# Softmax over rows of 1024: which queue issues each store

## The chip, the cores and the metric

The kernel runs on one core of a Trainium2 chip. The metric is the device time of one execution in microseconds (us). The kernel before takes 317.09 us, the median of three runs (316.88 to 317.21).

The core has several engines, each with an instruction queue of its own. VectorE (DVE in the profile) does reductions and elementwise arithmetic, ScalarE (ACT) the exponentials, GpSimd (POOL) next to nothing here, and SyncE (SP) only issues transfers. ACT, Pool and SP can all issue a DMA transfer between the chip's main memory (HBM) and the on-chip memory (SBUF). Each of the three has a DMA queue, which the profile calls q10, q0 and q1; the transfers of all three are carried by the same 16 DMA engines.

## The reference

The input x is 32 x 512 x 1024 in float32, so 16384 rows of 1024 numbers; `temperature` is 0.5. Each row goes through a softmax:

```
scaled = x / temperature
shifted = scaled - np.max(scaled, axis=-1, keepdims=True)
exp_x = np.exp(shifted)
return exp_x / np.sum(exp_x, axis=-1, keepdims=True)
```

Input and output are 67.11 MB each, and each is moved once.

## The kernel before

The rows are cut into 11 tiles. In a tile every one of the 128 partitions holds k whole rows of 1024 numbers side by side: k is 11 for tile 0, 12 for tiles 1 to 9 and 9 for tile 10 (`PASSES`, line 10). A transfer of a tile moves 128 pieces, one per partition, of 44 to 48 KB (36 KB for tile 10). Within a tile the rows are worked on in groups: 4, 4 and 3 in tile 0, two groups of 6 in each of tiles 1 to 9, and 4, 3 and 2 in tile 10. That makes 24 groups.

Each group goes through these steps, all in place in the tile:

- `maximum` (line 63): DVE takes the maximum of each row (line 69) and turns it into a bias (line 72).
- `exponential` (line 74): ACT computes exp of the scaled and shifted row, one instruction per row, and sums it as it goes (line 78).
- `divide` (line 87): DVE takes the reciprocal of the sums (line 90) and multiplies. In tiles 2, 3, 4, 6 and 8 (`WHOLE`) one instruction does the whole group (line 93), in the others there is one instruction per row (line 96).
- `store` (line 100): after the last group of a tile, the whole tile is sent to HBM by one transfer (line 108), and the next load is issued (line 109, line 60).

The order is written out by hand (`manual_schedule`, line 113): the instructions of each engine stand in its queue in the order in which the loop emits them. For each group g the loop emits its maximum and its exponentials, and then the divide and the store of group g - 1. So on DVE the divide of a group stands behind the maximum of the next group, and on ACT a store stands behind the exponentials of the next group. From tile 9 on (`ALONE`), the first group of a tile is preceded by the divide and the store of the group before.

There are four buffers for tiles (`BUFS`). Four loads are issued at the start, all by SP, and the load of tile i + 4 has to wait until the store of tile i has landed. All loads are on SP's queue, in order.

The stores of tiles 0 to 5 are issued by Pool and those of tiles 6 to 10 by ACT (`BY_POOL`, line 107). Ahead of the store of tile 0, Pool copies one column of tile 2 into a small tile `seen` that nothing reads (line 106). That copy waits for the load of tile 2, so the first store is issued only after this load has landed.

Of the kernel before, what the change touches and what calls it, by code (L numbers as in the profile page):

```python
# [1 line left out]

# [4 lines left out]

PASSES = [[4, 4, 3]] + [[6, 6]] * 9 + [[4, 3, 2]]  # L10
BUFS = 4

WHOLE = (2, 3, 4, 6, 8)


BY_POOL = 6

ALONE = 9


@with_exitstack
def kernel(
    ctx: ExitStack,
    tc: tile.TileContext,
    x: bass.AP,
    temperature: bass.AP,
    out: bass.AP,
):
    nc = tc.nc
    f32 = mybir.dt.float32  # L30
    scale = 1.0 / float(temperature)
    extreme = mybir.AluOpType.max if scale > 0 else mybir.AluOpType.min

    P = 128
    xf = x.flatten_outer_dims()
    of = out.flatten_outer_dims()
    n, d = xf.shape
    rows = [sum(ks) for ks in PASSES]
    assert sum(rows) * P == n

    data = ctx.enter_context(tc.tile_pool(name="data", bufs=BUFS))
    stats = ctx.enter_context(tc.tile_pool(name="stats", bufs=4))


    groups = []
    for i, ks in enumerate(PASSES):
        for j, k in enumerate(ks):
            groups.append((i, sum(ks[:j]), k))

    def dram(t, i):  # L50
        block = t[P * sum(rows[:i]) : P * sum(rows[: i + 1]), :]
        return block.rearrange("(p k) d -> p k d", p=P, k=rows[i])

    tiles, small = [], []

    def load():
        i = len(tiles)
        if i < len(PASSES):
            xt = data.tile([P, rows[i], d], f32, name="xt")
            nc.sync.dma_start(out=xt, in_=dram(xf, i))  # L60
            tiles.append(xt)

    def maximum(g):
        i, a, k = groups[g]
        top, bias, sums, recip = (
            stats.tile([P, k], f32, name=name) for name in ("top", "bias", "sums", "recip")
        )
        small.append((bias, sums, recip))
        nc.vector.tensor_reduce(  # L69
            out=top, in_=tiles[i][:, a : a + k, :], axis=mybir.AxisListType.X, op=extreme  # L70
        )
        nc.vector.tensor_scalar_mul(bias, in0=top, scalar1=-scale)  # L72

    def exponential(g):
        i, a, k = groups[g]
        bias, sums, _ = small[g]
        for b in range(k):
            nc.scalar.activation(  # L78
                tiles[i][:, a + b, :],
                tiles[i][:, a + b, :],  # L80
                mybir.ActivationFunctionType.Exp,
                bias=bias[:, b : b + 1],
                scale=scale,
                accum_out=sums[:, b : b + 1],
            )

    def divide(g):
        i, a, k = groups[g]
        _, sums, recip = small[g]
        nc.vector.reciprocal(recip, sums)  # L90
        if i in WHOLE:
            xt = tiles[i][:, a : a + k, :]
            nc.vector.tensor_mul(xt, xt, recip.unsqueeze(2).to_broadcast([P, k, d]))  # L93
            return
        for b in range(k):
            nc.vector.tensor_scalar_mul(  # L96
                tiles[i][:, a + b, :], in0=tiles[i][:, a + b, :], scalar1=recip[:, b : b + 1]
            )

    def store(g):  # L100
        i, a, k = groups[g]
        if a + k == rows[i]:
            if i == 0:


                nc.gpsimd.tensor_copy(stats.tile([P, 1], f32, name="seen"), tiles[2][:, 0, 0:1])  # L106
            queue = nc.gpsimd if i < BY_POOL else nc.scalar
            queue.dma_start(out=dram(of, i), in_=tiles[i])  # L108
            load()

    with tc.manual_schedule():
        for _ in range(BUFS):
            load()
        for g in range(len(groups) + 1):

            alone = g < len(groups) and groups[g][0] >= ALONE and groups[g][1] == 0
            if g > 0 and alone:
                divide(g - 1)  # L120
                store(g - 1)
            if g < len(groups):
                maximum(g)
                exponential(g)
            if g > 0 and not alone:
                divide(g - 1)
                store(g - 1)


# [1 line left out]
_INS = ['x', 'temperature']  # L131
_OUTS = [((32, 512, 1024), 'float32')]

_NUMBERS = {'temperature': 0.5}


# [26 lines left out]
```

## Time and profile before

| | us |
|---|---|
| median of three timed runs | 317.09 |
| span of the profiled execution, first to last instruction | 316.0 |
| DVE busy | 257.3 (81%) |
| ACT busy | 148.4 (47%) |
| POOL busy | 3.7 (1%) |
| one load of 6144 KB, issue to landing (median) | 36.4 |
| one store of 6144 KB by Pool, issue to landing (median) | 36.6 |
| one store of 6144 KB by ACT, issue to landing (median) | 33.1 |
| store of tile 10 (4608 KB) by ACT, issue to landing | 14.1 |

The profile shows one execution. The only time it gives for that execution is its span; the 1.1 us between the span and the median lie outside the first and the last instruction. Times within the profile count from the start of the span. Lines of the timeline give start, length, engine, line, operation, output and input; the bracket at the end tells how long the engine was idle before and what ended that. A letter q behind an engine's name (ACTq, SPq) marks its queue at the moment it issues a transfer; the length there is that of the issue, not of the transfer. Lines of the chain give start, length and what was worked on. DMA share and GB/s are those of the 16 DMA engines together; a packet counts where it starts, so short stretches scatter around the true rate.

### The profile page before, as it was taken

The numbers are of one execution on the slowest core, as the hardware profiler recorded it, in microseconds if no ns is written. First come the engines' busy times: TensorE is split into PE (matmuls) and PEld (weight loads), VectorE is DVE, ScalarE is ACT, GpSimd is POOL, SyncE is SP. The second block draws the span as 40 slices with busy tenths as digits, with TensorE's granted clock in tenths as the row PEclk, the third lists the DMA queues.
The fourth block names the chain that finished last, engine by engine and source line by source line (L and its number), as shares of the span: only waits on it lengthen the run. The fifth ranks groups of instructions, "written<-read, shape, count | busy, mean of one in ns | idle before, by whom it ended". The sixth has DMA issues, their size and how long they took to land.

```text
span 316.0 us, 529 instructions
## 1 busy us (share of the span) xinstructions
DVE 257.3 (81%) x150; ACT 148.4 (47%) x257; POOL 3.7 (1%) x11
## 2 busy tenths in 40 slices
DVE  0099999999999699979949993997399999888900
ACT  0048477468174444717181771447154705916600
POOL 0000010000000000000000000000000000000000
DMA  9999999999999999999999999999999999999995
GB/s 365 402 460 398 473 423 370 394 468 396 485 404 411 485 398 429 468 404 454 436 404 473 417 404 479 411 412 473 411 423 460 411 448 420 428 478 417 398 465 238
DMA packets 3171, 134.24 MB, mean 425 GB/s; under 512 B 352, under 2 KB 352, under 8 KB 352
## 3 DMA queue, kind: packets, MB, share of 16 engines
q1 hardware_dynamic: 1584, 67.11, 49.7%
q0 software_dynamic: 864, 37.22, 27.2%
q10 hardware_dynamic: 720, 29.88, 21.9%
q14 instruction: 3, 0.02, 0.0%
HBM read 67.11 MB, written 67.11 MB: 425 GB/s over the span
## 4 chain that ended last, share of the span: by engine, by line
DMA 47%; DVE 29%; ACT 10%; issue 9%; DVEq 0%; SPq 0%; POOLq 0%
DMA xt<-in_x_dram 24%; DMA out_dram<-xt 23%; DVE top L69 17%; ACT xt L78 10%; DVE xt L96 9%; DVE xt L93 2%; DVE bias L72 1%; DVE recip L90 0%; DVEq L158 0%; SPq L60 0%; POOLq L108 0%
## 5 line engine op out<-in xcount | busy, mean ns | idle before, releaser
L78 ACT ACTIVATE xt<-xt,bias 128x1024 f32<-128x1024 f32 x128 | 145.2, 1135 | 134.4 <-DVE recip L90 73.2
L69 DVE TENSOR_REDUCE top<-xt 128x6 f32<-128x6144 f32 (+3 forms) x24 | 140.1, 5836 | 36.9 <-DMA xt<-in_x_dram 36.9
L93 DVE TENSOR_TENSOR xt<-xt,recip 128x6144 f32<-128x6144 f32 x10 | 65.6, 6558 | 0.6 <-DVE recip L90 0.2
L96 DVE TENSOR_SCALAR xt<-xt,recip 128x1024 f32<-128x1024 f32 x68 | 46.3, 749 | 0.5
L78 ACT ACTIVATION_READ_ACCUMULATOR xt<-xt,bias 128x1 f32 x128 | 23.9, 186 | 0.0
L78 ACT ACT_TABLE_LOAD x1 | 1.3, 1283 | 16.4 <-DMA xt<-in_x_dram 16.4
L90 DVE RECIPROCAL recip<-sums 128x6 f32<-128x6 f32 (+3 forms) x24 | 4.3, 181 | 4.8 <-ACT xt L78 4.8
L108 POOL DMA_DIRECT2D out_dram<-xt x6 | 3.3, 555 | 128.9 <-ACT xt L78 83.7
L72 DVE TENSOR_SCALAR bias<-top 128x6 f32<-128x6 f32 (+3 forms) x24 | 4.1, 171 | 0.8
L106 POOL COPY seen<-xt 128x1 f32<-128x1 f32 x1 | 0.2, 185 | 45.0 <-DMA xt<-in_x_dram 45.0
L144 POOL MEMSET const-bfloat16-1.0<- 128x1 bf16 x1 | 0.1, 102 | 0.0
L144 POOL MEMSET const-uint8-127<- 128x1 uint8 x1 | 0.1, 102 | 0.0
L144 POOL MEMSET const-float32-0.0<- 128x1 f32 x1 | 0.1, 99 | 0.2 <-issue 0.2
L144 POOL MEMSET const-float32-1.0<- 128x1 f32 x1 | 0.1, 99 | 0.0
## 6 DMA issues: line engine op xcount, KB each, us to landing
xt<-in_x_dram SPq DMA_DIRECT2D x9, 6144.0 KB, 36.4
out_dram<-xt POOLq DMA_DIRECT2D x5, 6144.0 KB, 36.6
out_dram<-xt ACTq DMA_DIRECT2D x4, 6144.0 KB, 33.1
xt<-in_x_dram SPq DMA_DIRECT2D x1, 5632.0 KB, 15.6
out_dram<-xt POOLq DMA_DIRECT2D x1, 5632.0 KB, 29.2
xt<-in_x_dram SPq DMA_DIRECT2D x1, 4608.0 KB, 36.3
out_dram<-xt ACTq DMA_DIRECT2D x1, 4608.0 KB, 14.1
```

What stands on the lines that cost most here:

```text
L69: nc.vector.tensor_reduce(out=top, in_=tiles[i][:, a : a + k, :], axis=mybir.AxisListType.X, op=extreme)
L72: nc.vector.tensor_scalar_mul(bias, in0=top, scalar1=-scale)
L78: nc.scalar.activation(tiles[i][:, a + b, :], tiles[i][:, a + b, :], mybir.ActivationFunctionType.Exp, bias=bias[:, b : b + 1], scale=scal ...
L90: nc.vector.reciprocal(recip, sums)
L93: nc.vector.tensor_mul(xt, xt, recip.unsqueeze(2).to_broadcast([P, k, d]))
L96: nc.vector.tensor_scalar_mul(tiles[i][:, a + b, :], in0=tiles[i][:, a + b, :], scalar1=recip[:, b : b + 1])
L106: nc.gpsimd.tensor_copy(stats.tile([P, 1], f32, name="seen"), tiles[2][:, 0, 0:1])
L108: queue.dma_start(out=dram(of, i), in_=tiles[i])
L144: nc = _bacc.Bacc("TRN2", target_bir_lowering=False, num_devices=1)
```

## The change

Only the choice of the queue for each store changes, and the copy goes away. ACT issues the stores of tiles 0, 2, 4, 6 and 10, Pool those of tiles 1, 3, 5, 7, 8 and 9. The store of tile 0 is issued by ACT, without Pool's copy of a column of tile 2 ahead of it. Loads, groups, arithmetic and buffers are as before.

```diff
-BY_POOL = 6
+BY_POOL = (1, 3, 5, 7, 8, 9)
...
     def store(g):
         i, a, k = groups[g]
         if a + k == rows[i]:
-            if i == 0:
-
-
-                nc.gpsimd.tensor_copy(stats.tile([P, 1], f32, name="seen"), tiles[2][:, 0, 0:1])
-            queue = nc.gpsimd if i < BY_POOL else nc.scalar
+            queue = nc.gpsimd if i in BY_POOL else nc.scalar
             queue.dma_start(out=dram(of, i), in_=tiles[i])
             load()
```

## The prediction

> **What bounds the kernel now.** I read the page's busy row first, then its slices, then the stretches of the trace.
>
> ```profile
> span 316.0 us, 529 instructions
> DVE 257.3 (81%) x150; ACT 148.4 (47%) x257; POOL 3.7 (1%) x11
> DMA  9999999999999999999999999999999999999995
> q1 hardware_dynamic: 1584, 67.11, 49.7%
> q0 software_dynamic: 864, 37.22, 27.2%
> q10 hardware_dynamic: 720, 29.88, 21.9%
> ```
>
> The DMA row has no slice below nine tenths but the last: the 16 DMA engines are the bound. Queue q1 is SP's (loads), q0 Pool's, q10 ACT's. The stretches say how fast they go (start and end, length, DVE, ACT, POOL busy, then DMA share and GB/s):
>
> ```profile
> 16.00:46.00 30.00, 29.20 (x23) 18.28 (x30) 0.18 (x1) 1.00 0.97 421
> 46.00:48.00 2.00, 2.00 (x1) 2.00 (x5) 0.67 (x1) 1.00 0.92 393
> 48.00:50.00 2.00, 2.00 (x1) 0.58 (x2) 0.00 (x0) 1.00 1.54 393
> 50.00:52.00 2.00, 1.93 (x6) 1.41 (x3) 0.00 (x0) 1.00 0.78 338
> 52.00:60.00 8.00, 8.00 (x6) 5.49 (x10) 0.00 (x0) 1.00 0.93 401
> 100.00:200.00 100.00, 85.41 (x36) 47.39 (x84) 1.60 (x3) 1.00 1.00 433
> 200.00:300.00 100.00, 88.16 (x63) 51.70 (x90) 0.00 (x0) 1.00 1.00 433
> 312.00:316.00 4.00, 0.00 (x0) 0.00 (x0) 0.00 (x0) 1.00 0.13 55
> ```
>
> Saturated, they move 433 GB/s. The 134.22 MB need 310.0 us of that. SP issues at 0.74, the last store lands at 300.94 + 14.1 = 315.0, so at most some 5 us of 316.0 can be won. The only dip after the start is around 48 to 52, when the first store begins. In the packet records (8 packets per engine and transfer, 1.81 us each, 1.67 for tile 0) all 16 packets of load 3 that begin at 48.3 to 48.8 take 2.9 to 3.15 us, one 4.08: a **pause** of 1.2 us on 15 engines and 2.3 on one. Pool's first packets follow at 51.3. The engine with 4.08 ends last of all, at 314.74; the others end at 313.0 to 314.0, which is the thin last stretch, 312 to 316.
>
> The timeline shows the issues that the change touches:
>
> ```profile
> 45.46 0.18 POOL L106 COPY seen<-xt 128x1 f32<-128x1 f32 x1 [45.02 <-DMA xt<-in_x_dram]
> 46.04 0.67 POOL L108 DMA_DIRECT2D out_dram<-xt  x1 [0.39 <-issue]
> 65.86 0.53 POOL L108 DMA_DIRECT2D out_dram<-xt  x1 [19.16 <-DVE xt L96]
> ...
> 208.80 1.10 ACTq L108 DMA_DIRECT2D out_dram<-xt  x1
> 237.10 0.34 ACTq L108 DMA_DIRECT2D out_dram<-xt  x1
> 300.94 0.34 ACTq L108 DMA_DIRECT2D out_dram<-xt  x1
> ```
>
> And the chain shows the tail: load 8 lands at 226.1, and from there DVE and ACT work without a gap to the last divide.
>
> ```profile
> 187.96 38.14 DMA xt<-in_x_dram
> 226.09 0.02 issue
> 226.12 6.56 DVE top L69
> ...
> 282.21 4.34 DVE top L69
> ...
> 299.49 0.75 DVE xt L96
> ```
>
> The last store's first packet leaves at 302.4, when tile 9's store ends. SP's first load took 1.0 us from issue to first packet (0.74 to 1.73), so the issue at 300.94 is only about 0.5 us early.
>
> **The change part by part.** Bytes, loads and all DVE and ACT arithmetic stay; 11 stores stay 11. Pool issues six (0.53 each) before and after, ACT five (1.10 the first, 0.34 the others).
>
> *The copy (0.18 us at 45.46) and store 0 on ACT.* Pool loses a copy and the 0.39 gap: off the path, zero. Tile 0's last divide ends at 43.84; Pool issued at 46.04. ACT's queue holds six exponentials of tile 1 ahead of the store, which run to 48.6. That the issue can run ahead of queued exponentials is seen at 237.10, where two more start later (237.46, 238.59). Bounds: 43.9 to 48.6 for the issue, so 2.2 us earlier to 2.5 later. I take 46, as before: nine instructions are still queued at 43.84, five were at 237.10. What waits behind the store on ACT is tile 1's second group, released by DVE at 50.6, so neither the wait nor the first issue's 1.10 us costs anything. DMA is covered either way by load 3 (queued, landing at about 71). On SP, load 4 waits for store 0 (issued at 75.31); the store shifts it by at most the same 2.5 us while store 1 keeps the engines full. Without that cover each us would count in full. Zero.
>
> *The pause.* It goes with a store's first start. Three readings: it belongs to the first write of all (it stays, with store 0), to Pool's queue being used first (it moves to store 1, issued at 65.86), or to any start of Pool's queue from empty. Before, that happened once: stores 1 to 5 were appended to a busy q0, and 100:200, with three such issues, ran at 433. An empty q10 was first used at 208.80 with no dip (433 in 200:300). Bounds: it vanishes, -1.9 (below), or it comes at four starts, at stores 1, 3, 5 and 7 (8 and 9 are appended), +3.6 to +6.8. I take one pause, the single count that the trace shows: -1.2 + 1.2 = 0.
>
> *Stores 1 to 7 alternate.* The order of transfers could change now, since two stores may share the engines with a load. From issue to landing the trace gives 29.2, 34.7, 36.8, 36.6, 36.6, 41.4, 35.4 us for stores 0 to 6, so each next store is issued 9.4, 7.7, 7.5, 7.5, 10.4, 10.0 and 7.1 us before the one ahead lands. A store on an empty queue needs time to its first packet: 5.2 (store 0), 6.3 (store 6, beside two queues), 3.8 (load 4, beside one). The last packet ends 1 to 4 us before the landing. So the stores would meet for 0 to 3 us, and store 6 after store 5, already on another queue, met it for none: it started at 215.07, where q0 ended at 214.85. Work is conserved: at 98.4, where store 1's packets ended, stores 0 and 1 are done in both kernels with the same share of load 4. Bounds: from half a packet gained for loads (-0.9) to one packet lost (+1.81). I take zero, by the nearest row, store 6.
>
> *Stores 7, 8 and 9 from ACT to Pool.* Pool's issue has no queue ahead of it; ACT's came at the end of the divide too (237.10, 257.57, 282.24). ACT loses 3 x 0.34 us, idle time. 8 and 9 are queued behind a running store for 14 and 7 us. Zero.
>
> The row that bears on Pool's part is DVE's: right after 65.86, 122.15, 177.39, 237.10 and 257.57 it runs reductions of 6.5 us each, after 282.24 of 7.9, not divides. The Trainium skill (SBUF — State Buffer, "SBUF: two separate sides") warns that descriptors of a Pool-issued DMA can't be written while DVE runs a two-port operation, and recommends ACT's or SP's queue. By that rule alone, as an estimate, a start would wait for up to one divide run (4.07 us, L96), and with each of four Pool starts exposed the time would be 333; by the row the cost is zero, since reductions follow each issue and loads fill the wait.
>
> *Store 10* stays on ACT; store 9 ahead of it is now on another queue. It was queued before store 9 ended; now it interleaves with it, and the same bytes end together. Zero, at most +1.0 if its start is late by that first-packet time.
>
> Sum against the profiled execution: 316.0 + 0 = 316.0. The median, 317.09, is 1.1 above this span; I take that as unchanged: **317.1**.
>
> **The rivals.**
>
> *Pool's queue pauses at each start.* Place: stores 3, 5 and 7, beside store 1. Price 1.2 each on a saturated engine: +3.6, 320.7; if one engine were hit by 2.3 each time, +6.8, 323.9. For it: only Pool's queue showed a pause at a start; q10 and q1 (79.1) started from empty without. Against: one instance, and it was also the first write. It decides from the second pause on. Chance 0.27.
>
> *The pause goes away.* All engines end 1.2 earlier and the straggler no longer lags: the end falls from 314.74 to 313.98 - 1.2 = 312.8, so -1.9, 315.2. For it: queues ACT and SP have none. Against: Pool's queue still has its first use, at store 1. Chance 0.20. If it stays but hits all engines alike, the end is 313.98: -0.8, 316.3; chance 0.06.
>
> *Stores run ahead of loads.* If at stores 4 and 5 (10.4 us of early issue, the largest) a store takes one packet's turn from the loads and gives none back, load 8 lands 1.81 later, the gapless tail moves with it, and after 0.5 of slack the end is 1.3 later: 318.4. It decides from 0.5 us. Against: the gap after each store hands the turns back. Chance 0.09.
>
> *It does not do what it says:* store 0 waits for the exponentials and leaves at 48.6, later than Pool's. Price zero, as above; it is inside the forecast.
>
> **How the numbers follow.** Forecast 0.38: 317.1, own range 316.4 to 317.9, of which 0.30 within 0.2% (0.63 us, about what a measurement of this kernel can tell), 0.04 each side. Faster: 0.20 + 0.06 + 0.04 = 0.30. Slower: 0.27 + 0.09 + 0.04 = 0.40. The range reaches the case without a pause, 315.2 less 0.4 for a fully even end, and the case of four pauses with one uneven hit, 320.7 + 1.1: 314.8 to 321.8.
>
> **What would show it.** q0 with 864 packets and 37.75 MB, q10 720 and 29.36 MB; no copy on Pool; store 0 issued by ACT between 43.9 and 48.6. One dip below 433 GB/s in 46 to 80 and none in 100:300 is the forecast; dips near 127, 182 and 242 are the first rival; no dip the second. Load 8 landing later than 226.6 is the third. Wrong also if SP's loads wait for more than before: load 4 issued later than 78, with a stretch in 68 to 90 below 425.

## The result, and the profile after

The changed kernel takes 320.42 us (median of six runs, 319.49 to 322.55) against 317.15 for the kernel before: a ratio of 1.0109 (95% interval 1.008 to 1.0137). It is slower by about 1.1%, and its runs scatter over 3 us where those of the kernel before lie within 0.5. In the larger series beside the experiments the kernel before scatters too: of 29 runs beside runs 5 to 7 most lie near 317.3, and six between 318.8 and 320.3.

The page of the changed kernel, its busy row, its slices and its queues:

```profile
span 318.0 us, 525 instructions
DVE 257.3 (81%) x150; ACT 148.5 (47%) x257; POOL 3.5 (1%) x10
DMA  9999998999999999999999999999999999999976
q1 hardware_dynamic: 1584, 67.11, 49.5%
q0 software_dynamic: 864, 37.75, 27.5%
q10 hardware_dynamic: 720, 29.36, 21.4%
```

The arithmetic is the same to 0.1 us, and the queues carry just the bytes that were foreseen. What is new stands at the end of the DMA row: 7 and 6 instead of 9 and 5. Stretches (start and end, length, DVE, ACT, POOL busy, DMA share, GB/s) of the kernel before:

```profile
46.00:60.00 14.00, 13.93 (x10) 9.48 (x18) 0.67 (x1) 1.00 0.99 390
100.00:200.00 100.00, 85.41 (x36) 47.39 (x84) 1.60 (x3) 1.00 1.00 433
200.00:300.00 100.00, 88.16 (x63) 51.70 (x90) 0.00 (x0) 1.00 1.00 433
300.00:304.00 4.00, 0.91 (x2) 0.00 (x0) 0.00 (x0) 1.00 1.10 476
304.00:308.00 4.00, 0.00 (x0) 0.00 (x0) 0.00 (x0) 1.00 0.98 424
```

and of the changed kernel:

```profile
46.00:60.00 14.00, 13.93 (x10) 9.71 (x18) 0.00 (x0) 1.00 1.04 427
100.00:200.00 100.00, 81.17 (x36) 47.50 (x84) 1.06 (x2) 1.00 1.00 433
200.00:300.00 100.00, 89.09 (x56) 49.32 (x86) 1.59 (x3) 1.00 1.00 429
300.00:304.00 4.00, 3.58 (x8) 2.38 (x4) 0.00 (x0) 1.00 0.65 283
304.00:308.00 4.00, 0.79 (x2) 0.00 (x0) 0.00 (x0) 1.00 0.69 295
```

From 100 to 200 us the engines are as full as before. From 300 to 308 they move 283 and 295 GB/s: most of them have run out of work, because the last store is not there yet. Its first packets start at 305.7, while store 9's end between 302.0 and 305.5, depending on the engine. The last store's issue, and DVE's wait for loads, in the changed kernel:

```profile
304.82 0.34 ACTq L104 DMA_DIRECT2D out_dram<-xt  x1
```

```profile
DVE top L69 <- DMA xt<-in_x_dram: 40.9, 6, 16.6
```

and DVE's wait in the kernel before:

```profile
DVE top L69 <- DMA xt<-in_x_dram: 36.9, 6, 16.4
```

Before, the last store was issued at 300.94. So its issue is now 3.9 us later, and DVE waits 4.0 us more. The chain of the changed kernel's end tells which load it was:

```profile
213.10 39.29 DMA out_dram<-xt
...
252.48 33.44 DMA xt<-in_x_dram
285.91 0.02 issue
285.94 4.43 DVE top L69
```

Store 6, issued at 213.10, lands at 252.4; only then is the load of tile 10 issued, and it lands at 285.9, against 280.6 before. DVE is idle there and takes up tile 10 at once. Before, DVE came to tile 10 at 282.2 and the load had been there for 1.6 us.

The lateness can be followed further back. DVE's first maximum of tile 7 waits for load 7, and store 6 goes out only after that maximum and one divide. Before:

```profile
195.28 6.55 DVE L69 TENSOR_REDUCE top<-xt 128x6 f32<-128x6144 f32 x1 [4.83 <-DMA xt<-in_x_dram]
208.80 1.10 ACTq L108 DMA_DIRECT2D out_dram<-xt  x1
```

In the changed kernel:

```profile
199.57 6.55 DVE L69 TENSOR_REDUCE top<-xt 128x6 f32<-128x6144 f32 x1 [8.19 <-DMA xt<-in_x_dram]
213.10 0.34 ACTq L104 DMA_DIRECT2D out_dram<-xt  x1
```

Load 7 lands 4.3 us later, so store 6 goes out 4.3 later. Store 6 then takes 39.3 us instead of 35.4; store 7, now on the other queue, starts at 239.6, while store 6's packets run to 246.2 (run 2 tests this pair). Load 10 takes 33.4 us instead of 36.3. Together it lands 5.3 later, of which 1.6 was to spare.

The store of tile 0, in the timeline of ACT:

```profile
44.10 0.37 ACTq L104 DMA_DIRECT2D out_dram<-xt  x1
```

It went out 1.9 us before Pool's (46.04), past eight instructions of ACT that had not begun. Its first packets start at 49.0 instead of 51.3.

In the profiled runs where the time of the execution itself is known, about 1.8 us lie outside the span (319.78 - 318.0 here), and in all the timed runs of the kernel before, beside the experiments, 1.7 to 1.8 do (317.38 with a span of 315.6). So the execution of before that was profiled took some 317.8 us, about 0.6 more than the median of 317.15, and the 1.1 us between its span and the median of 317.09 mix two different executions. With this the 2.0 us between the spans and the 3.3 between the medians nearly agree: the execution of the changed kernel that was profiled took 319.78, some 0.6 less than its median.

Two things had to be told apart: the alternation of the queues (theory M: stores that meet, that is, move at the same time on two queues, take turns from the loads), and the first store without the copy. From each profile I took four numbers out of the packet records: the start of store 0's first packet; the number of slow packets (over 0.1 us longer than their kind, between 75 and 285 us, out of some 1,900); and, from the landings, when load 10 is complete and how far its 16 engines lie apart. Each row's profile is one execution, which need not be a typical one of its kernel (run 6: 321.45 with a median of 320.58; run 8: 317.25, its lowest). The median and the ratio are of 6 to 12 timed runs. The ratio sets a kernel against runs of the kernel before taken beside it. It lies close to the ratio of the means, in which stray runs count, so ratio and median can differ: run 6 is 3.1 us slower by its median and 1.9 by its ratio. Runs over 1.5% above the fastest of their kernel (four in run 2, two in run 6, one in run 7) are in the medians and not in the ratios. "Held" means that the first store waits.

| run | median us | ratio | 95% interval | store 0 starts | slow packets | load 4 issued | load 10 lands (spread) | last store issued |
|---|---|---|---|---|---|---|---|---|
| before | 317.2 to 317.4 | 1 | | 51.3 | 6 | 75.3 | 280.6 (1.7) | 300.9 |
| changed kernel | 320.42 | 1.0109 | 1.008 to 1.0137 | 49.0 | 48 | 78.2 | 285.9 (5.3) | 304.8 |
| 1: store 0 by ACT | 320.3 | 1.0071 | 1.004 to 1.0101 | 48.8 | 48 | 78.1 | 285.3 (6.5) | 304.1 |
| 2: 7, 8, 9 back to ACT | 319.27 | 1.004 | 1.0013 to 1.0067 | 48.8 | 36 | 78.2 | 281.7 (4.8) | 300.9 |
| 3: before, 7, 8, 9 by Pool | 318.28 | 1.0023 | 1.0011 to 1.0034 | 51.2 | 7 | 74.7 | 284.4 (3.9) | 303.3 |
| 4: all by ACT | 320.16 | 1.0082 | 1.0052 to 1.0112 | 48.7 | 30 | 74.3 | 281.1 (4.6) | 300.1 |
| 5: store 0 by ACT, held | 319.52 | 1.0051 | 1.0025 to 1.0077 | 51.3 | 14 | 80.7 | 283.7 (4.8) | 302.9 |
| 6: before without the copy | 320.58 | 1.0059 | 1.0024 to 1.0095 | 48.8 | 32 | 74.5 | 286.1 (9.3) | 305.0 |
| 7: alternation, Pool's copy kept | 318.53 | 1.0016 | 0.999 to 1.0043 | 51.0 | 8 | 74.9 | 282.2 (1.6) | 301.1 |
| 8: copy replaced by a delay | 317.59 | 1.002 | 0.9997 to 1.0042 | 51.3 | 8 | 75.0 | 280.2 (1.3) | 300.8 |
| 9: copy and a delay | 318.01 | 1.0022 | 1.0001 to 1.0043 | 53.1 | 10 | 75.2 | 280.5 (1.6) | 301.1 |
| 10: all by ACT, held | 318.46 | 1.0025 | 1.0008 to 1.0042 | 51.3 | 11 | 75.3 | 279.8 (2.7) | 299.9 |
| 11: a small write at the start | 318.28 | 1.0041 | 1.0024 to 1.0059 | 51.4 | 12 | 74.9 | 281.9 (1.5) | 302.4 |
| 12: changed kernel, held | 320.79 | 1.0108 | 1.0072 to 1.0144 | 51.3 | 6 | 80.9 | 286.8 (7.9) | 305.7 |

### The profile page after: what moved, and what is told of

Same layout as the page of the kernel before. It is cut to its first block, busy times and chain, and to the rows that moved or that the text cites. A ratio compares the mean times of both kernels' runs of the same rounds, so it can differ in the third digit from the quotient of the medians.

```text
span 318.0 us, 525 instructions
## 1 busy us (share of the span) xinstructions
DVE 257.3 (81%) x150; ACT 148.5 (47%) x257; POOL 3.5 (1%) x10
## 6 DMA issues: line engine op xcount, KB each, us to landing
xt<-in_x_dram SPq DMA_DIRECT2D x1, 4608.0 KB, 33.4
out_dram<-xt ACTq DMA_DIRECT2D x1, 4608.0 KB, 12.3
```

## Experiments: which part of the change

**Run 1, store 0 by ACT alone.**

```diff
-BY_POOL = (1, 3, 5, 7, 8, 9)
+BY_POOL = (1, 2, 3, 4, 5)
```

> The first part of the change alone: no copy on Pool, the store of tile 0 by ACT; 1 to 5 by Pool and 6 to 10 by ACT as before. Theory M (stores that meet on two queues take turns from the loads, the last load lands late, and the last store starts late): stores 1 to 5 are in one queue, 6 to 10 in another, so nothing new meets; 316.3 to 317.3, load of tile 10 lands near 280.6, last store issued near 301, one pause near 47 of under 1 us. Theory F (the earlier first store costs the 3 us): 319.5 or more.

320.3 us (317.51 to 322.13), 1.0071 against 1.0109 for the changed kernel: most of the loss is there although stores 1 to 5 are in one queue and 6 to 10 in another. So theory M falls for the later stores. It does not fall for the first two: the expectation overlooked that store 0 on ACT and store 1 on Pool meet here as well, and load 4 is issued at 78.1, as in the changed kernel.

**Run 2, the late stores back to ACT.**

```diff
-BY_POOL = (1, 3, 5, 7, 8, 9)
+BY_POOL = (1, 3, 5)
```

> As the changed kernel, but the stores of tiles 7, 8 and 9 go back to ACT, so that store 7 queues behind store 6. Theory M, with stores 6 and 7 as the pair that matters (they met from 239.6 to 246): load of tile 10 lands by 282, the last store is issued by 302, 316.5 to 317.8. If the pair 4 and 5 matters as much: 318 to 319. Theory P (six stores on alternating queues cost, whoever issues the late ones): 319.5 to 321.

In the profiled execution (319.04) the load of tile 10 lands at 281.7 and the last store is issued at 300.9, both as theory M has it with the pair 6 and 7, but the time is 319.27 (317.23 to 324.15), above its 316.5 to 317.8. That execution ends late while a few DMA engines lag: the landings of load 10 spread over 4.8 us and those of the last store over 3.0. Store 6 takes 32.6 us here instead of 39.3, now that store 7 queues behind it. The pair 6 and 7 is a part, not the whole.

**Run 3, the late stores by Pool, everything else as before.**

```diff
-BY_POOL = 6
+BY_POOL = (0, 1, 2, 3, 4, 5, 7, 8, 9)
-            queue = nc.gpsimd if i < BY_POOL else nc.scalar
+            queue = nc.gpsimd if i in BY_POOL else nc.scalar
```

> As the kernel before, with Pool's copy, but the stores of tiles 7, 8 and 9 by Pool. Theory M: store 7 is issued near 237 and starts near 242.3, where store 6 ends in the kernel before (242.0), so little meets: 316.8 to 318. Theory Q (Pool's queue itself is slower late in the kernel, as the longer packets at 245 to 262 might say): 319 to 321, with the same longer packets.

318.28 (318.0 to 318.77), 1.0023. The runs lie close together and the longer packets at 245 to 262 are gone, so theory Q falls. Moving the late stores costs some 0.9 us by itself (0.7 by the ratio): store 7 starts at 241.7, store 6 lands at 245.6, load 10 lands at 284.4 and the last store goes out at 303.3.

**Run 4, all stores by ACT.**

```diff
-BY_POOL = (1, 3, 5, 7, 8, 9)
+BY_POOL = ()
```

> All eleven stores by ACT, one queue, no copy. Theory M: no two stores meet, 316 to 317.3, load of tile 10 lands by 281.5. Theory P: the same as M here. Theory F (early first store): 319.5. If Pool's queue is what takes the time around the span, the time outside the span is below the 1.8 us of the changed kernel.

320.16 (317.88 to 321.81). Here no two stores can meet, and Pool issues none. The last store goes out at 300.1, earlier than before, yet the time is nearly that of the changed kernel: 30 slow packets, and the landings of load 10 spread over 4.6 us. The time outside the span is 1.8 us here too, so Pool's queue isn't what takes it. What runs 1, 2, 4 and the changed kernel share is the early first store.

## Experiments: the first store's moment

**Run 6, the kernel before without its copy.**

```diff
-            if i == 0:
-                nc.gpsimd.tensor_copy(stats.tile([P, 1], f32, name="seen"), tiles[2][:, 0, 0:1])
```

> The kernel before without Pool's copy: Pool issues the first store as soon as the divide ends, near 43.9. Theory W: 316.8 to 317.8, as before, with the pause of 1.2 us. Theory X: 319 to 321, pause below 1 us, single slow packets later.

320.58 (316.75 to 323.22). One copy of one column, and nothing else, is worth 3 us in the median and 1.9 by the ratio (0.8 to 3.0). Who issues is not the point (theory W falls). Pool's line in this run:

```profile
44.53 0.67 POOL L104 DMA_DIRECT2D out_dram<-xt  x1 [44.08 <-DVE xt L96]
```

**Run 8, the copy replaced by a delay.**

```diff
-                nc.gpsimd.tensor_copy(stats.tile([P, 1], f32, name="seen"), tiles[2][:, 0, 0:1])
+                late = stats.tile([P, 512], f32, name="late")
+                nc.gpsimd.tensor_copy(late, tiles[0][:, 10, 0:512])
+                nc.gpsimd.tensor_copy(late, tiles[0][:, 10, 512:1024])
```

> The kernel before with Pool's copy of tile 2 replaced by two copies of 512 columns of tile 0 to a scratch tile, which wait for the divide and not for a load: the first store leaves 1 to 3 us after 43.9, about when the kernel before lets it go (46.0). Theory T (what matters is the moment of the first store): 316.8 to 317.8 and single runs within 1 us if it is issued at 45.5 or later. Theory L (what matters is that load 2 has landed first, whatever the moment): if it is issued before 45.4, 319 to 321; if after, as T.

317.59 (317.25 to 320.23), 1.002 with an interval that holds 1. The median is that of theory T. Its runs were to lie within 1 us and do not: three of twelve are above 319, where the series of the kernel before beside it has one of 29. The timeline of Pool:

```profile
44.24 0.61 POOL L107 COPY late<-xt 128x512 f32<-128x512 f32 x1 [43.80 <-DVE xt L96]
44.91 0.61 POOL L108 COPY late<-xt 128x512 f32<-128x512 f32 x1
45.47 0.66 POOL L110 DMA_DIRECT2D out_dram<-xt  x1
```

The store leaves 0.9 us later than in run 6, and its first packets start one packet of load 3 later (51.3 instead of 48.8). It leaves before load 2 has landed on all engines (45.8), so the wait for load 2 isn't needed; the moment is. By the ratios alone runs 6 and 8 are not clear of each other (their intervals overlap between 1.0024 and 1.0042); runs 4 and 10, below, are.

**Run 9, later still.** The two copies stand behind the copy of tile 2.

```diff
                 nc.gpsimd.tensor_copy(stats.tile([P, 1], f32, name="seen"), tiles[2][:, 0, 0:1])
+                late = stats.tile([P, 512], f32, name="late")
+                nc.gpsimd.tensor_copy(late, tiles[0][:, 10, 0:512])
+                nc.gpsimd.tensor_copy(late, tiles[0][:, 10, 512:1024])
```

> The kernel before with its copy and the two copies of 512 columns behind it: the first store leaves 1 to 3 us later than 46.0. Theory T: one packet of load 3 more goes ahead, engines stay in step, 316.8 to 317.8; if the moment has to be just that of the kernel before, 318 to 321. The store's later start itself costs nothing while load 3 keeps the DMA engines busy.

318.01, store 0 starts at 53.1, another packet later: 10 slow packets. A later start does little harm (0.6 us in the median, at the edge of what these runs tell); an earlier one does more.

**Run 10, all by ACT, but held.** An exponential of one column stands ahead of the store in ACT's queue and has to wait for load 2. The store goes out at 45.93, just after load 2 has landed (45.90), and the exponential itself runs only at 48.97: what holds the store is the wait, not the work.

```diff
-BY_POOL = 6
+BY_POOL = ()
-                nc.gpsimd.tensor_copy(stats.tile([P, 1], f32, name="seen"), tiles[2][:, 0, 0:1])
+                nc.scalar.activation(
+                    stats.tile([P, 1], f32, name="seen"),
+                    tiles[2][:, 0, 0:1],
+                    mybir.ActivationFunctionType.Exp,
+                    scale=scale,
+                )
```

> All eleven stores by ACT, the first behind a one-column exponential of tile 2 on ACT (issued near 45.9, first packets near 51.3). One queue, so no two stores meet. Theory T: 316 to 317.5, single runs within 1 us, against 320.2 for the same without the wait. Theory W (Pool must issue the first store): 319 to 321.

318.46 (318.09 to 319.1) against 320.16 for run 4: 11 slow packets instead of 30, and runs within 1 us. The two intervals (1.0008 to 1.0042 and 1.0052 to 1.0112) do not overlap, and the wait is the only difference between the two kernels: on ACT's queue the moment of the first store matters. The time is 1 us above what was expected: at the end of the profiled execution the landings still spread over 2.7 us.

**Run 11, a small write at the start.**

```diff
     with tc.manual_schedule():
+        first = stats.tile([P, 128], f32, name="first")
+        nc.gpsimd.memset(first, 0.0)
+        nc.scalar.dma_start(out=dram(of, 10)[:, 0, 0:128], in_=first)
```

> The kernel before, with one small write of 512 bytes per partition to the rows of tile 10 of the output, issued by ACT at the very start (tile 10's store overwrites it at the end). It takes the first write away from the first store and leaves that store's moment, 46.0. Theory 1 (the pause belongs to the first write of the execution): no pause near 48, about 1.2 us less where the engines stay in step, 315.8 to 316.6. Theory 2 (the pause belongs to the start of stores beside a load, or to Pool's queue): the pause stays, 317.2 to 317.8. Theory S (it is the pause of 1.2 us that lines the engines up, and without it they fall out of step as in the runs without the copy): no pause, single slow packets along the run, 318 to 321.

The pause stays (the packets of load 3 just before the first store take 2.6 to 3.1 us), so it isn't the first write's. The time is 318.28: theory 1 and theory S fall, and the extra write gains nothing. Theory 2 is right about the pause, but the time is above its range too; why the small write costs some 1 us (1.0024 to 1.0059) is open.

## Experiments: the first pair of stores

**Run 5, store 0 by ACT, held; the rest as before.** 
```diff
-BY_POOL = 6
+BY_POOL = (1, 2, 3, 4, 5)
-                nc.gpsimd.tensor_copy(stats.tile([P, 1], f32, name="seen"), tiles[2][:, 0, 0:1])
+                nc.scalar.activation(
...
+                    tiles[2][:, 0, 0:1],
...
-            queue = nc.gpsimd if i < BY_POOL else nc.scalar
+            queue = nc.gpsimd if i in BY_POOL else nc.scalar
```

> The first store by ACT, but behind a one-column exponential of tile 2 on ACT that takes the place of Pool's copy: the store is issued at 45.5 or later instead of 44.3. All other stores as in the kernel before. Theory W (what matters is that Pool's queue issues the first store): 319.5 to 321, slow packets of single engines all along the run, landings of late loads spread over 3 us or more. Theory X (what matters is that the first store starts later, a packet further into load 3): 316.5 to 317.6, spread under 2 us.

319.52 (318.02 to 320.83), 14 slow packets. It differs from run 10 in that stores 1 to 5 are on Pool's queue, so store 1 needn't queue behind store 0: its first packets start at 70.7 instead of 73.7, store 0 lands at 80.6 instead of 75.2, and load 4 is issued at 80.7 instead of 75.3. Time and spread are those of theory W, but its slow packets are not there (14, where the early starts have 30 to 48). That the 2 us (1.6 by the ratio) come from the pair is a guess here: the intervals of runs 5 and 10 overlap, and stores 2 to 5 changed their queue too. Runs 7 and 12 test it.

**Run 7, the alternation with Pool's first store.**

```diff
-BY_POOL = 6
+BY_POOL = (0, 1, 3, 5, 7, 8, 9)
```

> The whole alternation, but the first store by Pool with its copy, as before: Pool issues 0, 1, 3, 5, 7, 8, 9, ACT 2, 4, 6, 10. Theory W and X alike (the first store is what matters): 317.5 to 318.8, as the run with only 7, 8 and 9 moved (318.3), and a spread of single runs below 1 us. Theory M (alternation): 319.5 to 321.

318.53, eleven of twelve runs between 317.97 and 319.79, one at 324.16. Stores 0 and 1 are in one queue here, load 4 is issued at 74.9, and all the later alternation costs about 1 us in the median, 0.5 by the ratio, whose interval holds 1. Run 7 differs from the changed kernel in store 0 alone, which Pool issues behind its copy. So the larger part of the change's loss (1.0109 against 1.0016, with intervals that do not overlap) hangs on store 0: on who issues it and on its wait.

**Run 12, the changed kernel, held.**

```diff
+            if i == 0:
+                nc.scalar.activation(
+                    stats.tile([P, 1], f32, name="seen"),
+                    tiles[2][:, 0, 0:1],
+                    mybir.ActivationFunctionType.Exp,
+                    scale=scale,
+                )
```

> The changed kernel, with the first store on ACT held back by the one-column exponential of tile 2 (issued near 45.9, first packets near 51.3). If the moment of the first store is most of the change's loss: 318 to 319, like the alternation behind Pool's copy (318.5). If the alternation is most of it: 320 to 321, like the changed kernel. If the first pair matters (store 1 on Pool meets store 0 on ACT and load 4 is issued near 80 instead of 75, as in the run where ACT waits): 319 to 320.

320.79 (320.33 to 323.16). The first of the three expectations, 318 to 319, falls: the wait alone wins nothing back, although slow packets are down to 6. By the number it is the second, the alternation. But run 7 has all the later alternation and takes 318.53, so what is left is the pair of stores 0 and 1 on two queues, together with the later alternation; alone (run 5) the pair cost less. Run 10 rules out that a held store 0 on ACT costs this much by itself. DVE's wait for loads in run 12:

```profile
DVE top L69 <- DMA xt<-in_x_dram: 41.7, 7, 16.9
```

Run 7, where stores 0 and 1 share Pool's queue:

```profile
DVE top L69 <- DMA xt<-in_x_dram: 36.7, 6, 16.8
```

5 us less, as in the kernel before (36.9). The chain of run 12 has the same end as the changed kernel's, the load of tile 10 behind store 6:

```profile
214.22 34.62 DMA out_dram<-xt
...
248.92 37.87 DMA xt<-in_x_dram
286.79 0.02 issue
286.81 4.43 DVE top L69
```

So the loss has two sources, and they don't add up. Starting store 0 at 49 instead of 51.3 costs time (runs 4 and 10, and less clearly 6 and 8), and the profiles of early starts have many slow packets. Putting store 1 on another queue than store 0 costs time where the later stores alternate too (runs 12 and 7), and makes store 0 land up to 6 us later, so that load 4 goes out up to 6 us later. The changed kernel has both: 48 slow packets, and load 4 issued at 78.2. Holding the store removes the first and worsens the second (80.9). No run beats the kernel before.

What stays open: why a start one packet earlier is followed by so many slow packets. With one profile for each kernel, it isn't shown either that they belong to the kernel and not to the one execution; none of the long executions of the kernel before (318.8 to 320.3) was profiled. The records show that the slow ones are mostly reads of single engines, all along the run, and that the order of transfers is the same to 0.5 us in run 6 and in the kernel before (load 4's first packet 78.7 and 79.1, load 6's 136.8 and 137.1). A pause before the first store is there in all runs, so its absence isn't the cause. But it is uneven in the early starts: the last packets of load 3 before the store are longer by 0.4 to 1.1 us in the changed kernel, 0.0 to 0.7 in run 4 and 0.1 to 1.3 in run 6, depending on the engine, and by 0.9 to 1.4 on every engine in runs 5, 8, 9, 10 and 12. Runs 3, 7 and 11, with few slow packets as well, lie between (0.5 to 1.4). Whether this puts the engines out of step is not shown.

Open too is the way from the first pair to the late load 10. It is not simply the late load 4: in run 5 load 4 goes out 5.4 us late, and load 7 lands at 195.2 all the same, as in the kernel before. With the later alternation load 7 lands at 198.4 in run 7, 199.6 in the changed kernel and 200.7 in run 12, so run 7, which loses little, has much of this lateness too.

## Why the prediction was right or wrong

The measured 320.42 lies in the range (314.8 to 321.8). Slower was given 0.40, more than the other two signs, but the forecast was 317.1, and the rival that names nearly the measured time (320.7, Pool's queue pauses at each start) is not the cause. The range reached that far up only for four pauses, which did not come. That it held the time was luck: the sum had zero for every part, and the loss came from parts at zero.

- *"Zero" for the copy and store 0 on ACT* is the step that failed. The issue came at 44.10, next to the early end of my bounds (43.9); I took 46, on the ground that nine instructions were still queued. The cover was argued from bytes: load 3 keeps the engines busy. That held (46 to 80 moves 424 GB/s, 423 before). The price is elsewhere: run 6 moves this moment alone by 1.5 us and costs 3.1 us in the median, 1.9 by the ratio; and with store 0 on ACT and store 1 on Pool, holding the store wins nothing back (run 12). The prediction let the issue move 2.2 us earlier or 2.5 later and put a price of zero on both ends, because it counted bytes. Whether the 16 engines stay in step had no term.
- *One pause* was right in number and wrong in place. It stayed with store 0 instead of moving to Pool's first use, and it is shorter: the packets of load 3 before it take 2.2 to 3.0 us instead of 2.9 to 4.1 (427 GB/s in 46 to 60 against 390). No pause stands at Pool's starts near 129, 183 and 240 (the stretch 100:200 is at 433, and no packet that starts from 232 to 244 is over 0.1 us longer than its kind), so the first rival falls by its own sign. Its other reading, the first write, falls by run 11.
- *Alternation of stores 1 to 7 at zero, between -0.9 and +1.81*: with stores 0 and 1 in one queue it measured 0.5 us by the ratio (run 7, interval from -0.3 to +1.4) and 1.1 in the median, inside the bounds. Store 6 after store 5 was the wrong row for the first pair. There store 1 meets store 0 for 4.3 us (71.5 to 75.8 in the changed kernel). I had counted an early issue of 9.4 us and subtracted a start of 5.2 and a lag of 1 to 4 us between the last packet and the landing; for store 0 that lag is 0.4 us (74.87 to 75.24 before). Work was conserved at 98.4, as I had it: 80 of load 4's 128 packets were done in both kernels. But store 0, which load 4 waits for, landed 2.9 us later, and that had no price.
- *Stores 7 to 9 at zero*: 0.9 us in the median, 0.7 by the ratio (run 3). Pool's queue had no delay that matters, as DVE's row said; the cost is that store 7 no longer queues behind store 6, and load 10 lands 3.8 later.
- *Store 10 at zero, at most +1.0*: its issue moved by 3.9 us in the profile, and the end of the span by 2.0. So the slack in the tail was not 0.5 us but 1.8: the last store takes 12.3 us instead of 14.1, since it no longer waits for store 9's packets and its 16 engines start together (landings 0.2 us apart, 1.7 before).
- *The rival "stores run ahead of loads"* (0.09, 318.4) had the end of the chain right: late load, gapless tail, last store late, engines idle. It put it at stores 4 and 5 and at load 8, with one packet's price of 1.3. It came at load 10, issued behind store 6: the last store went out 3.9 us later. Load 8 landed at 223.7, earlier than before, so its stated sign (load 8 after 226.6) was wrong.
- *What would make it wrong* named load 4 issued later than 78: it was issued at 78.2. The low stretch named with it is not there as stated: 68 to 90 moves 450 GB/s, and it is the kernel before that has 424 there. Low is 60 to 80, with 422 GB/s (446 before).
- *The median at 1.1 above the span, "unchanged"* compared two executions: about 1.8 us lie outside the span, and the profiled execution of before took some 0.6 us more than the median.

The Trainium skill's warning on Pool-issued transfers beside DVE (SBUF — State Buffer, "SBUF: two separate sides"), which would have made 333 as an estimate, isn't seen in these runs. DVE is in reductions or idle after each of Pool's issues in the changed kernel, so they did not put it to the test. There Pool's stores on an empty queue (1, 3, 5, 7) had their first packets 4.4 to 5.4 us after the issue, ACT's (0, 2, 4, 6) 3.4 to 5.4.

## What to carry to other kernels

In a kernel that keeps the DMA engines full, bytes and bandwidth don't decide the last percent: what decides is which transfer is complete when, since a transfer lands with the slowest of its 16 engines (load 10 of the changed kernel: 5.3 us after the fastest). Where consecutive stores on two queues meet, the second takes turns from the first, and what waits for the first (here the next load) goes out later, as load 4 did by 5.4 us in run 5. Where they hardly met, in run 7, alternation cost little. Before a wait that looks idle is dropped, run the kernel with that wait alone removed.

## What was not expected of the hardware

- 0.9 us in the issue of one store (44.53 in run 6, 45.47 in run 8) changes the median by 3.0 us and the scatter of twelve runs from 6.5 to 3.0 us; by the ratios it is 1.2 us, and their intervals overlap.
- A DMA issue on ACT's queue went out with eight of ACT's instructions ahead of it not yet begun (44.10 in the changed kernel, where the last of them starts at 48.62).
- Load packets are held up by 0.4 to 1.3 us on all 16 engines just before the first full store begins, whichever queue issues it (ACT in the changed kernel and run 10, Pool in runs 8 and 9), with a small write long before it too (run 11); in runs 4 and 6 the delay is uneven, and near zero on some engines. Later starts of stores in the changed kernel show none.
- Engines can drift apart: in run 4 the landings of a load spread over 0.8 us at load 3, 2.9 at load 7 and 4.6 at load 10. It isn't a one-way road: in run 7 the spread is 2.4, 2.8 and 1.6 us.
